# Hybrid decoder trunk: two score blocks ahead of the first gate part in the mixer's written order, other pieces moved by one place, input blocks in other tiles

## The chip, the cores and the metric

The kernel runs on one core of a Trainium2 chip. Its engines are TensorE (PE, matrix products into PSUM), VectorE (DVE) and ScalarE (ACT), GpSimd (POOL) and SyncE (SP), which here issues most DMA transfers. Each engine works through its own instruction queue in order and waits on semaphores of the others. The metric is the device time of one execution in microseconds (us), the median of the runs; lower is better.

## The reference

A two-layer decoder trunk on one sequence of 512 tokens and 1024 channels. Layer 0 mixes tokens with a diagonal state-space model (S5) on half of the projected channels and with stick-breaking attention (8 heads of 64) on the rest. Layer 1 is a convolution module. Each layer ends with a feed-forward net. The change touches the mixer of layer 0 alone:

```python
h = x @ mix_w_in[i] + mix_b_in[i]
u, q, k, v = jnp.split(h, [S5_WIDTH, S5_WIDTH + SB_WIDTH, S5_WIDTH + 2 * SB_WIDTH], axis=-1)
s5_out = s5_mixer(u, ...)
sb_out = stick_breaking_attention(q.reshape(head_shape), k.reshape(head_shape), v.reshape(head_shape))
mix = jnp.concatenate([s5_out, sb_out], axis=-1) @ mix_w_out[i] + mix_b_out[i]

# stick_breaking_attention, for each block of 128 queries
z = jnp.einsum('bqhd,bkhd->bhqk', q_blk, kf) * scale
log_beta = jax.nn.log_sigmoid(z)
log_keep = jnp.where(strict, jax.nn.log_sigmoid(-z), 0.0)
after = lax.cumsum(log_keep, axis=3, reverse=True) - log_keep
weights = jnp.where(strict, jnp.exp(log_beta + after), 0.0)
out = jnp.einsum('bhqk,bkhd->bqhd', weights, vf)

# s5_mixer: bu = u times b_bar, a causal scan of complex states, then
y = jnp.real(jnp.einsum('blgn,gpn->blgp', states, c))
y = jax.nn.gelu(y + d * u)
val, gate = jnp.split(y @ w_glu + b_glu, 2, axis=-1)
return val * jax.nn.sigmoid(gate)
```

## The kernel before

**Numbers.** Each large product is split into three: weights and inputs are cut into a high part (`whi`, `xh`, made by ACT) and a low part (`wlo`, `xl`, made by DVE as the difference), and PE multiplies high by high, high by low and low by high. A weight piece of 128 x 1024 numbers comes by DMA into `raw` (two buffers), then ACT casts it (L117 or L114) and DVE subtracts (L118 or L115). Three pieces may be ready at a time.

**Start.** Eight blocks of the input, `xin0` to `xin7`, are loaded into tiles that later serve others (tags "spt", "wt", "q", "k"), and PE turns them. Then come the four projections u0 to u3. Each leaves PSUM by an ACT copy `ue` (L652) into a tile of tag "wt" and goes through DRAM into `U`. Meanwhile ACT and DVE compute four sine and cosine tables (`tables`, L505 to L522): ACT writes `fa` and `fb`, DVE reduces them in four steps (L390, L514, L515, L390 and L517), and ACT takes Sin, Abs and Sin (`ts`, `fb`, `tc`). After the last Sin ACT loads another table set, for Exp and Ln.

**The mixer's order.** From there PE follows the list `ORDER` (L62): each word names a piece, and every PE instruction is tied behind the one before it (L844). DVE's, ACT's and SP's queues are not written by hand; the framework's scheduler puts them together from that program and its priorities. The words are:

- `q0`, `k0`, `v0` and so on: projections of 24 products of 512 columns, one pair of heads each. An ACT copy takes each out of PSUM.
- `G0` to `G3` (`s5_tables`): the gate part of the S5 model. DVE builds `Gx` and `Cx`; PE turns `Gx` (`gp`, two blocks) and multiplies (`tp`); ACT copies these out as `gt`, `gt` and `tk`; sixteen small DMA transfers put `tk` into `Tx`.
- `s0` to `s3` (`s5_states`): PE multiplies `vR` and `vI` from `gt` and `U`, DVE forms the states with the tables and two scans and writes `Sx`.
- `y0` to `y3` (`s5_outputs`): PE makes `yp` from `Tx`, `Cx` and `Sx`, and DVE adds it to `U` in four pieces. `Cx` for the next part may be written only when `yp` has read it.
- `a0sB`: score block B of head pair 0 (`z0B`, both heads), followed by its softplus: ACT takes Abs, Exp and Ln, DVE finishes `sp`, ACT casts `sh`, DVE subtracts `sl`. C and A likewise; C is half as wide.
- `a0t`: v0 turned (`vt`, copied out by ACT). `a0wB0`: the weights of block B, head 0, 8 products on `z0B`, and an Exp on ACT (`w0B`). `a0vC`: the values of block C, into the one buffer "av". `a0e`: that buffer is taken out (`ch` by ACT, `cl` by DVE), which frees it for the next pair.
- `e0`: the GELU of part 0. `r`, `R`: rows of bias vectors. `l0`, `o0`: the gated linear unit and the output product.

**Buffers.** In PSUM three buffers of tag "mm" go round over the projections, `gp`, `gp`, `tp`, `vt`, `vR`, `vI` and `yp` in the order of the program, so each of these waits until the third one back has been read; four of tag "z" hold scores, one "av". In SBUF the tiles "spt" and "wt" have three buffers each, "q" and "k" two.

Of the kernel before, what the change touches and what calls it, by code (L numbers as in the profile page):

```python
# [12 lines left out]
AF = mybir.ActivationFunctionType  # L13
# [43 lines left out]
MIX_BUFS = (3, 4, 1, 3, 3)  # L57
WARM = 24
QK_BUFS = (2, 2, 1, 1)
SP_BUFS = {"A": 1, "B": 2, "C": 2}  # L60
TABLES_FIRST = (0, 1, 2, 3)
ORDER = "q0 k0 v0 G0 s0 a0sB a0sC a0t q1 k1 y0 a0wB0 a0wC0 a0wC1 a0wB1 a0sA a0vC r G1 s1 a0wA0 v1 a0wA1 a0vB a1sC a1sB y1 q2 a0vA a1wC0 a1wC1 e0 G2 a1sA s2 k2 a1wB0 a0e a1t v2 a1wB1 a1vC y2 a1vB e1 a1wA0 a2sB a1wA1 q3 a1vA a1e e2 G3 a2sC s3 k3 a2wB1 a2t a2wC0 a2wC1 a2vC a2sA a2wB0 R y3 e3 v3 a3sC a2wA0 a2vB a2wA1 a3sB l0 a2vA a2e a3wC0 a3wC1 l1 a3t a3sA a3wB1 l2 l3 a3wA0 a3vC a3wB0 a3wA1 o0 o1 o2 o3 o4 o5 a3vB a3vA a3e o6 o7".split()  # L62


class Weights:
# [100 lines left out]
def units_of(name, w, k0, nk, cols, width):  # L166

    ncol = 1024 // nk
    out = []
    for c in cols:  # L170
        base = c // width * width
        src = w[k0 * P : (k0 + nk) * P, base : base + width].rearrange("(k p) n -> p k n", p=P)
        out.append(((name, k0, base), src, nk, ncol, c - base, width))
    return out
# [29 lines left out]
def kernel(ctx: ExitStack, tc: tile.TileContext, a: dict, out: bass.AP):  # L204
    nc = tc.nc
    act = Act(tc)
# [42 lines left out]
    def pv(n, i):  # L249
        if n == "mix_b_in":  # L250
            return PB[:, i : i + 1]
        return PV[:, vrow[n] + i : vrow[n] + i + 1]
# [25 lines left out]
    units = units_of("u", w_in, 0, 8, range(0, 512, 128), 128)  # L278
    for o in ORDER:
        if o[0] in "qkv":  # L280
# [38 lines left out]
    xin = []  # L319
    with tc.high_priority():  # L320
        for j in range(KT):
            tag, bufs = (("spt", MIX_BUFS[3]), ("wt", MIX_BUFS[4]), ("q", QK_BUFS[0]), ("k", QK_BUFS[1]))[(0, 1, 0, 1, 0, 1, 3, 2)[j]]
            xt = att.tile([P, 4, P], F32, tag=tag, name=f"xin{j}", bufs=bufs)
            nc.sync.dma_start(xt, a["x"][0][:, P * j : P * (j + 1)].rearrange("(b p) f -> p b f", p=P))
            xin.append(xt)
# [26 lines left out]
    for j in range(KT):  # L352
        ps = (mm if j % 2 else s5ps)(f"xT{j}")
# [275 lines left out]
    def c_states(last):  # L629
        with tc.issue_after(last):  # L630
            for i in range(2):
                cp = zz(f"cp{i}")
                for b in range(4):
                    PE.transpose(cp[:, b * P : (b + 1) * P], Craw[i][:, b, :], ident)
                cv = cp.rearrange("p (r g q) -> p r g q", g=2, q=16)
                for h in range(2):
                    hp = slice(h * 64, h * 64 + 64)
                    V.tensor_copy(Cd[hp, i], cv[hp, :, h, :])

    def in_proj(tile_i, name):  # L640
        w = W.next()
        ps = mm(name)
        proj_last[:] = [gemm(ps, w, slice(0, P), xs, 0, T)]
        return ps, pv("mix_b_in", tile_i)

    Ud = [tc.dram_tile([P, T], F32, name=f"Ud{j}") for j in range(4)]
    for j in range(4):
        ps, b = in_proj(j, f"u{j}") if j else (u0, pv("mix_b_in", 0))
        if j == 1:
            c_states(proj_last[0])  # L650
        up = att.tile([P, T], F32, tag="wt", name=f"ue{j}", bufs=MIX_BUFS[4])
        act(up.rearrange("p (t c) -> p c t", t=4), ps.rearrange("p (c t) -> p c t", t=4), AF.Identity, bias=b)  # L652
        nc.sync.dma_start(Ud[j], up)
        for t in range(4):
            nc.sync.dma_start(U[32 * t : 32 * t + 32, 4 * j : 4 * j + 4, :],
                              Ud[j].rearrange("(r f) (t c) -> t f r c", r=4, t=4)[t])
# [177 lines left out]
    before, traced = None, nc.cur_bb.bb.instructions  # L834
    for o in ORDER:
        at = len(traced)
# [64 lines left out]
    for layer in range(2):  # L901
# [3 lines left out]
        k0 = 0  # L905
# [200 lines left out]
    for n in ("ln1_g", "ln2_g", "conv_ln_g"):  # L1106
        c = PV[:, vrow[n] : vrow[n] + a[n].shape[0] * KT]
# [31 lines left out]
    k0 = 0  # L1139
# [90 lines left out]
    ws, ps, last = [None] * KT, [None] * KT, {}  # L1230
# [129 lines left out]
    def rect(m, ps):  # L1360

        r = page(f"r1{m}", F32)
        act(r, ps, AF.Relu, bias=pv("ffn_b1", 32 + m))
        return r

    def hidden(m):

        ps = stp(f"f1{m}")
        gemm(ps, W.next(), slice(0, P), xs, 0, T)
        return ps  # L1370
# [49 lines left out]
    k0 = 0  # L1420
# [9 lines left out]
    for i in range(nb_last):  # L1430
        if i % 3 == 0:
            hl_ = [f1[f"a{i // 3}"].tile([P, 3, T], F32R, tag=f"a{x}", name=f"b{x}{i}", bufs=1) for x in "hl"]
        r = rect(k0 + i, hidden(k0 + i))
# [88 lines left out]
```

## Time and profile before

| What | Value |
|---|---|
| median of 3 runs | 1146.21 us (1146.03 to 1146.39) |
| the profiled execution | 1147.06 us |
| its span, from first to last instruction | 1145.3 us |
| mean granted TensorE clock | 0.997 |
| four projections u, from the first product | 8.2 to 34.6 us |
| the mixer's written order | 34.4 to 232.7 us |
| DVE busy in 40 to 60 us | 19.56 of 20 us |
| ACT busy in 40 to 60 us | 15.37 of 20 us |

Rows of the timeline give start, duration, engine, line, operation, output and inputs, shapes and, in square brackets, how long the engine was idle before it and what ended that. A matmul's duration contains its way through the array, so rows overlap, and the distance of two starts says more than a duration. In the table of waits each row is one engine and operation, what it waited for, the total, the number of waits and the longest.

### The profile page before, as it was taken

The numbers are of one execution on the slowest core, as the hardware profiler recorded it, in microseconds if no ns is written. First come the engines' busy times: TensorE is split into PE (matmuls) and PEld (weight loads), VectorE is DVE, ScalarE is ACT, GpSimd is POOL, SyncE is SP. The second block draws the span as 40 slices with busy tenths as digits, with TensorE's granted clock in tenths as the row PEclk, the third lists the DMA queues.
The fourth block names the chain that finished last, engine by engine and source line by source line (L and its number), as shares of the span: only waits on it lengthen the run. The fifth ranks groups of instructions, "written<-read, shape, count | busy, mean of one in ns | idle before, by whom it ended". The sixth has DMA issues, their size and how long they took to land.

```text
span 1145.3 us, 16443 instructions
## 1 busy us (share of the span) xinstructions
PE 1124.8 (98%) x6460; PEld 945.5 (83%) x6460; DVE 811.6 (71%) x1408; ACT 538.7 (47%) x814; POOL 39.7 (3%) x77
## 2 busy tenths in 40 slices
PE   9999999999999999999999999999999999999997
PEld 7777777799887888888899887699988888888885
DVE  7998875588745644645547899877795959588337
ACT  6966778435524524524513321354674535363530
POOL 1000000000000000000002211002000000000000
PEclk9999999999999999999999999999999999999999
DMA  9621221150878778788608586546043241515211
GB/s 206 172 66 49 73 70 66 58 181 32 269 242 281 245 255 292 267 277 303 228 6 290 205 252 197 163 121 221 1 129 93 84 136 45 158 37 159 72 46 74
DMA packets 152109, 175.35 MB, mean 153 GB/s; under 512 B 15522, under 2 KB 124834, under 8 KB 152032
## 3 DMA queue, kind: packets, MB, share of 16 engines
q1 hardware_dynamic: 143232, 142.81, 39.4%
q0 software_dynamic: 8640, 31.46, 8.1%
q8 instruction: 51, 0.84, 0.3%
q14 instruction: 26, 0.21, 0.1%
q10 hardware_dynamic: 160, 0.03, 0.0%
HBM read 132.25 MB, written 35.65 MB: 147 GB/s over the span
## 4 chain that ended last, share of the span: by engine, by line
PE 88%; DVE 4%; DMA 4%; ACT 3%; issue 1%; SPq 0%; DVEq 0%; ACTq 0%
PE f L265 24%; PE acf L265 11%; PE s L1407 10%; PE fl L265 6%; PE tlb L265 4%; PE tld L265 4%; PE h L1452 4%; PE pv L265 3%; PE pg L265 3%; PE cw L1200 2%; PE tla L265 2%; PE pl L265 2%; PE v L265 1%; PE acmo L265 1%; DMA raw<-in_mix_w_in_dram 1%; PE gg L265 1%
## 5 line engine op out<-in xcount | busy, mean ns | idle before, releaser
L117 ACT CAST whi<-raw 128x1024 fp32r<-128x1024 f32 (+1 forms) x150 | 157.1, 1061 | 261.3 <-PE acf L265 72.5
L118 DVE TENSOR_TENSOR wlo<-raw,whi 128x1024 fp32r<-128x1024 f32 (+1 forms) x150 | 183.9, 1237 | 120.8 <-ACT whi L117 120.5
L265 PE MATMUL f<-xah,whi 128*128 128x512 f32 x208 | 81.1, 390 | 0.0
L265 PE MATMUL f<-xal,whi 128*128 128x512 f32 x208 | 81.0, 390 | 0.0
L265 PE MATMUL f<-xah,wlo 128*128 128x512 f32 x208 | 80.9, 389 | 0.0
L265 PE MATMUL f<-xdh,whi 128*128 128x512 f32 x208 | 80.9, 389 | 0.0
L265 PE MATMUL f<-xdl,whi 128*128 128x512 f32 x208 | 80.9, 389 | 0.0
L265 PE MATMUL f<-xdh,wlo 128*128 128x512 f32 x208 | 80.9, 389 | 0.0
L265 PE MATMUL acf<-hh,whi 128*128 128x512 f32 x192 | 76.0, 396 | 0.0
L265 PE MATMUL acf<-hh,wlo 128*128 128x512 f32 x192 | 75.6, 394 | 0.0
L265 PE MATMUL acf<-hl,whi 128*128 128x512 f32 x192 | 75.1, 391 | 0.0
L1407 PE MATMUL s<-whi,al 128*128 128x512 f32 x168 | 65.0, 390 | 0.0
L1407 PE MATMUL s<-wlo,ah 128*128 128x512 f32 x168 | 65.0, 390 | 0.0
L1407 PE MATMUL s<-whi,ah 128*128 128x512 f32 x168 | 64.5, 392 | 0.0
L118 DVE TENSOR_TENSOR wlo<-quad,whi 128x1536 fp32r<-128x1536 f32 x28 | 49.1, 1755 | 7.6 <-ACT whi L117 7.3
L117 ACT CAST whi<-quad 128x1536 fp32r<-128x1536 f32 x28 | 41.0, 1483 | 17.2 <-PE f L265 8.0
L398 DVE SCALAR_TENSOR_TENSOR cy<-hp,wdw,cy 128x256 f32<-128x256 f32 (+1 forms) x80 | 46.2, 578 | 0.4 <-ACT cy L192 0.4
L265 PEld LDWEIGHTS f<-xal,whi 128*128 128x128 f32 x208 | 39.0, 188 | 8.1
L265 PEld LDWEIGHTS f<-xdh,wlo 128*128 128x128 f32 x208 | 39.0, 188 | 8.1
L265 PEld LDWEIGHTS f<-xdh,whi 128*128 128x128 f32 x208 | 39.0, 188 | 8.1
L265 PEld LDWEIGHTS f<-xah,wlo 128*128 128x128 f32 x208 | 39.0, 188 | 8.1
L265 PEld LDWEIGHTS f<-xdl,whi 128*128 128x128 f32 x208 | 39.0, 188 | 8.1
(649 smaller groups left out, 2979.4 us busy)
## 6 DMA issues: line engine op xcount, KB each, us to landing
raw<-in_ffn_w_dram SPq DMA_DIRECT2D x35, 1024.0 KB, 5.4
kepth<-whi SPq DMA_DIRECT2D x30, 512.0 KB, 2.8
keptl<-wlo SPq DMA_DIRECT2D x30, 512.0 KB, 3.7
whi<-kepth POOLq DMA_DIRECT2D x30, 512.0 KB, 4.2
wlo<-keptl POOLq DMA_DIRECT2D x30, 512.0 KB, 5.3
raw<-in_ffn_w_dram SPq DMA_DIRECT2D x28, 512.0 KB, 3.9
raw<-in_conv_w_pw_dram SPq DMA_DIRECT2D x12, 1024.0 KB, 7.3
quad<-in_ffn_w_dram SPq DMA_DIRECT2D x16, 768.0 KB, 4.2
```

The costliest lines, as they stand in the source:

```text
L117: i0 = nc.scalar.copy(hi, raw).ins
L118: i1 = nc.vector.tensor_sub(lo, raw, hi.bitcast(F32)).ins
L265: ins = PE.matmul(ps[:, c0:c1], u[:, k, ksl], v[:, c0:c1], start=start and k == 0 and i == 0, stop=stop and k == n - 1 and i == 2).ins
L398: V.scalar_tensor_tensor(o, x, s, y, op0=op0, op1=op1)
L1200: PE.matmul(cps[j, c0][32 * g : 32 * g + 32, c0:c1], Ws[j][:, 4 * b + g, :], Hs[j, c0][g][:, 4 * b : 4 * b + c1 - c0], start=b == 0, stop= ...
L1407: PE.matmul(ps, u, v[:, p, :], start=chain == i and p == 0 and n_ == 0, stop=p == len(As) - 1 and n_ == 2, skip_group_check=True)
L1452: PE.matmul(ps, u, v, start=k == 0 and i == 0, stop=k == nb_last - 1 and i == 2)
```

## The change

Three edits. The list `ORDER` is changed in six places: the score blocks `a0sB a0sC` go ahead of `G0`, and `a0t` ahead of `s0`; `v1` goes ahead of `s1` and `a0wA0`; `q2` ahead of `y1`; `a0e` directly behind `a0vA`; and in the third pair `a2vC` goes behind `a2sA a2wB0`. Of the line the diff shows what moves. The input blocks use other tile tags. The ACT copy `ue` gets the scheduler's high priority.

```diff
-ORDER = "q0 k0 v0 G0 s0 a0sB a0sC a0t q1 k1 y0 a0wB0 a0wC0 a0wC1 a0wB1 a0sA a0vC r G1 s1 a0wA0 v1 a0wA1 a0vB a1sC a1sB y1 q2 a0vA a1wC0 a1wC1 e0 G2 a1sA s2 k2 a1wB0 a0e a1t v2 a1wB1 a1vC y2 ... a2wB1 a2t a2wC0 a2wC1 a2vC a2sA a2wB0 R y3 ..."
+ORDER = "q0 k0 v0 a0sB a0sC G0 a0t s0 q1 k1 y0 a0wB0 a0wC0 a0wC1 a0wB1 a0sA a0vC r G1 v1 s1 a0wA0 a0wA1 a0vB a1sC a1sB q2 y1 a0vA a0e a1wC0 a1wC1 e0 G2 a1sA s2 k2 a1wB0 a1t v2 a1wB1 a1vC y2 ... a2wB1 a2t a2wC0 a2wC1 a2sA a2wB0 a2vC R y3 ..."
@@ the input blocks @@
-            tag, bufs = (("spt", MIX_BUFS[3]), ("wt", MIX_BUFS[4]), ("q", QK_BUFS[0]), ("k", QK_BUFS[1]))[(0, 1, 0, 1, 0, 1, 3, 2)[j]]
+            tag, bufs = (("spt", MIX_BUFS[3]), ("k", QK_BUFS[1]), ("q", QK_BUFS[0]), ("wt", MIX_BUFS[4]))[(0, 1, 0, 1, 0, 2, 2, 3)[j]]
@@ the projections u @@
-        act(up.rearrange("p (t c) -> p c t", t=4), ps.rearrange("p (c t) -> p c t", t=4), AF.Identity, bias=b)
+        with tc.high_priority():
+            act(up.rearrange("p (t c) -> p c t", t=4), ps.rearrange("p (c t) -> p c t", t=4), AF.Identity, bias=b)
```

Lines behind L652 stand one further down in the changed kernel. Numbers behind the names are buffers; the same tile can have another one in the changed program.

The first place is DVE's queue at the end of the sine tables, from the low part of q1's weights (`wlo_720`) to the last step of the fourth table (`fa_508`, L517). Before:

```order
L115 SCALAR_TENSOR_TENSOR wlo_720<-raw_717,whi_719 128x1024
L390 TENSOR_SCALAR fr_510<-fa_508 128x512
L394 TENSOR_TENSOR cm<-EE,Braw 128x256
L517 TENSOR_TENSOR fa_508<-fa_508,fr_510 128x512
L394 TENSOR_TENSOR cm<-EE,Braw 128x256
L394 TENSOR_TENSOR Gx<-cm 64x16x16 x2
L394 TENSOR_TENSOR cm<-PW,Cd 128x320 x2
L394 TENSOR_TENSOR Cx<-cm 64x20x16 x2
L118 TENSOR_TENSOR wlo_753<-raw_750,whi_752 128x1024
```

And in the changed kernel, where `fa_487` is the third table:

```order
L115 SCALAR_TENSOR_TENSOR wlo_720<-raw_717,whi_719 128x1024
L515 TENSOR_TENSOR fa_487<-fa_487,fb_488 128x512
L390 TENSOR_SCALAR fr_510<-fa_508 128x512
L390 TENSOR_SCALAR fr_489<-fa_487 128x512
L514 TENSOR_TENSOR fa_508<-fa_508,fr_510 128x512
L517 TENSOR_TENSOR fa_487<-fa_487,fr_489 128x512
L515 TENSOR_TENSOR fa_508<-fa_508,fb_509 128x512
L394 TENSOR_TENSOR Cx<-cm 64x20x16
L390 TENSOR_SCALAR fr_510<-fa_508 128x512
L394 TENSOR_TENSOR cm<-PW,Cd 128x320
L118 TENSOR_TENSOR wlo_753<-raw_750,whi_752 128x1024
L517 TENSOR_TENSOR fa_508<-fa_508,fr_510 128x512
```

The steps of the third and fourth table, which stood ahead of `wlo_720`, now stand behind it, and the last one also behind `wlo_753`; the `cm`, `Gx` and `Cx` work moved ahead instead.

The second place is ACT's queue from its table load to the copies of the first gate part (`gt`, `gt`, `tk`) and of the turned v0 (`vt`). Before:

```order
L194 ACT_TABLE_LOAD
L117 CAST whi_938<-raw_936 128x1024
L192 ACTIVATE v_781<-v_756,PB 128x512
L565 COPY gt_808<-gp_803 128x512
L565 COPY gt_815<-gp_810 128x512
L577 COPY tk_826<-tp_817 128x128
L192 ACTIVATE sp0B_886<-z0B_876 128x512
L192 ACTIVATE sp0B_896<-z0B_877 128x512
```

In the changed kernel, from v0's copy to the first of these copies and on to the second:

```order
L192 ACTIVATE v_781<-v_756,PB 128x512
L192 ACTIVATE sp0B_793<-z0B_783 128x512
L192 ACTIVATE sp0B_803<-z0B_784 128x512
L198 ACTIVATE sp0B_793<-sp0B_793 128x512
L198 ACTIVATE sp0B_803<-sp0B_803 128x512
L198 ACTIVATE sp0B_793<-sp0B_793 128x512
L198 ACTIVATE sp0B_803<-sp0B_803 128x512
L192 ACTIVATE sp0C_818<-z0C_812 128x256
L565 COPY gt_861<-gp_856 128x512
L255 CAST sh0B_799<-sp0B_793 128x512
L255 CAST sh0B_808<-sp0B_803 128x512
L198 ACTIVATE sp0C_818<-sp0C_818 128x256
```

The queue goes on there with:

```order
L565 COPY gt_868<-gp_863 128x512
L198 ACTIVATE sp0C_818<-sp0C_818 128x256
L192 ACTIVATE sp0C_827<-z0C_813 128x256
L577 COPY tk_879<-tp_870 128x128
L198 ACTIVATE sp0C_827<-sp0C_827 128x256
L255 CAST sh0C_823<-sp0C_818 128x256
L198 ACTIVATE sp0C_827<-sp0C_827 128x256
L700 COPY vt_902<-vt_897 128x512
```

The softplus of the two score blocks, which followed `tk`, now stands between v0's copy and the four copies.

The third place is DVE's queue around `yp1`, the second S5 output, up to the last `Cx` of the third part. Before:

```order
L394 TENSOR_TENSOR Cx<-cm 64x20x16
L398 SCALAR_TENSOR_TENSOR sp1B_1278<-z1B_1268,sp1B_1278 128x512
L398 SCALAR_TENSOR_TENSOR sp1B_1287<-z1B_1269,sp1B_1287 128x512
L398 SCALAR_TENSOR_TENSOR U<-U,par,yp_1296 128x128
L256 TENSOR_TENSOR sl1B_1284<-sp1B_1278,sh1B_1283 128x512
L256 TENSOR_TENSOR sl1B_1293<-sp1B_1287,sh1B_1292 128x512
L398 SCALAR_TENSOR_TENSOR U<-U,par,yp_1296 128x128 x3
L394 TENSOR_TENSOR Cx<-cm 64x20x16
L394 TENSOR_TENSOR cm<-PW,Cd 128x320 x2
L398 SCALAR_TENSOR_TENSOR Cx<-cm 64x20x16 x2
```

In the changed kernel, where `wlo_1502` is the low part of q3's weights and `cl_1349` that of pair 0's values:

```order
L398 SCALAR_TENSOR_TENSOR sp1B_1287<-z1B_1269,sp1B_1287 128x512
L115 SCALAR_TENSOR_TENSOR wlo_1502<-raw_1499,whi_1501 128x1024
L256 TENSOR_TENSOR sl1B_1293<-sp1B_1287,sh1B_1292 128x512
L394 TENSOR_TENSOR Cx<-cm 64x20x16
L398 SCALAR_TENSOR_TENSOR U<-U,par,yp_1329 128x128 x4
L256 TENSOR_TENSOR cl_1349<-av_1075,ch_1348 128x512
L394 TENSOR_TENSOR Cx<-cm 64x20x16
L394 TENSOR_TENSOR cm<-PW,Cd 128x320 x2
L398 SCALAR_TENSOR_TENSOR Cx<-cm 64x20x16 x2
```

The softplus of the second pair stood behind the first `Cx`, and now stands ahead of it, with the weights; `cl` has come in.

More of the change, by code (lines that the diff above doesn't have):

```diff
@@ L61 @@
 TABLES_FIRST = (0, 1, 2, 3)
-ORDER = "q0 k0 v0 G0 s0 a0sB a0sC a0t q1 k1 y0 a0wB0 a0wC0 a0wC1 a0wB1 a0sA a0vC r G1 s1 a0wA0 v1 a0wA1 a0vB a1sC a1sB y1 q2 a0vA a1wC0 a1wC1 e0 G2 a1sA s2 k2 a1wB0 a0e a1t v2 a1wB1 a1vC y2 a1vB e1 a1wA0 a2sB a1wA1 q3 a1vA a1e e2 G3 a2sC s3 k3 a2wB1 a2t a2wC0 a2wC1 a2vC a2sA a2wB0 R y3 e3 v3 a3sC a2wA0 a2vB a2wA1 a3sB l0 a2vA a2e a3wC0 a3wC1 l1 a3t a3sA a3wB1 l2 l3 a3wA0 a3vC a3wB0 a3wA1 o0 o1 o2 o3 o4 o5 a3vB a3vA a3e o6 o7".split()
+ORDER = "q0 k0 v0 a0sB a0sC G0 a0t s0 q1 k1 y0 a0wB0 a0wC0 a0wC1 a0wB1 a0sA a0vC r G1 v1 s1 a0wA0 a0wA1 a0vB a1sC a1sB q2 y1 a0vA a0e a1wC0 a1wC1 e0 G2 a1sA s2 k2 a1wB0 a1t v2 a1wB1 a1vC y2 a1vB e1 a1wA0 a2sB a1wA1 q3 a1vA a1e e2 G3 a2sC s3 k3 a2wB1 a2t a2wC0 a2wC1 a2sA a2wB0 a2vC R y3 e3 v3 a3sC a2wA0 a2vB a2wA1 a3sB l0 a2vA a2e a3wC0 a3wC1 l1 a3t a3sA a3wB1 l2 l3 a3wA0 a3vC a3wB0 a3wA1 o0 o1 o2 o3 o4 o5 a3vB a3vA a3e o6 o7".split()
 class Weights:
```

## The prediction

> **What bounds the kernel now.** I read the page first, then the list of what TensorE waited for, then engine timelines of the first 160 us, where every step of the change lies. All times are us from the start of the span unless a clock or a count is meant.
>
> ```profile
> PE 1124.8 (98%) x6460; PEld 945.5 (83%) x6460; DVE 811.6 (71%) x1408; ACT 538.7 (47%) x814; POOL 39.7 (3%) x77
> PE 88%; DVE 4%; DMA 4%; ACT 3%; issue 1%; SPq 0%; DVEq 0%; ACTq 0%
> ```
>
> The page says that TensorE (PE) is the bound: 98% busy, and 88% of the chain that ended last. Behind the mixer there is almost no idle time on it, so whatever shift the mixer has gathered when it ends arrives unchanged at the end of the span. The question is only how the mixer's PE queue shifts. PE works strictly in the written order there, so each of its waits counts in full.
>
> ```profile
> PE vR L588 <- ACT gt L565: 1.9, 1, 1.9
> PE tp L573 <- issue: 1.5, 1, 1.5
> PE v L265 <- ACT ue L192: 1.3, 1, 1.3
> PE av L760 <- DVE cl L256: 0.9, 1, 0.9
> PE av L760 <- ACT w2C L198: 0.9, 2, 0.5
> ```
>
> These five rows of the waits (engine, line, what it waited for; total, times, longest) are what the change can hope to take: 6.5 us in all. The opposite danger is in the table of windows, where VectorE (DVE) is full as well:
>
> ```profile
> 40.00:60.00 20.00, 17.26 (x106) 13.48 (x106) 19.56 (x37) 15.37 (x28) 0.99 (x1) 1.00 0.53 140
> ```
>
> The columns are stretch, length, busy time of PE, weight loads, DVE, ACT and POOL, then clock and DMA. DVE is busy 19.56 us of 20, and ACT and PE feed it. An order that lets DVE or ACT stand still here cannot be made good soon.
>
> **The wait for ue3, and what is late next.** The three "mm" buffers of PSUM go round, so v0 takes the one of u3 and waits until ScalarE (ACT) has copied ue3 out.
>
> ```profile
> 51.10 0.68 ACT L192 ACTIVATE k<-k,PB 128x512 f32<-128x512 f32 x1
> 54.83 0.73 PE L573 MATMUL tp<-Cx,Gx 128*32 128x128 f32 x16 [1.48 <-issue]
> 57.46 1.14 PE L718 MATMUL z0B<-q,k 64*128 64x384 f32 x8
> 60.03 0.62 PE L697 MATMUL vt<-ident,v 128*128 128x128 f32 x4
> 60.41 0.47 PE L265 MATMUL q<-x0h,whi 128*128 128x512 f32 x1
> ```
>
> With its high priority ue3 comes out several us before v0 asks for it, so v0 starts and ends 1.3 earlier. But behind v0 now stand the score blocks z0B and z0C, which read k0 from SBUF. ACT copies k0 out at 51.10 to 51.78, and in the new order no earlier, since that copy stands behind the third table's Sin. So z0B starts near 52.0, and most of the 1.3 comes back at once. The two score blocks (57.46 to 60.03, 2.6) then end near 54.6, the gate transposes gp near 55.6.
>
> **Trig tables later (the DVE place of the change section).** DVE's last subtraction for the fourth table (L517) is what ACT's last Sin waits for.
>
> ```profile
> 45.82 1.22 DVE L115 SCALAR_TENSOR_TENSOR wlo<-raw,whi 128x1024 fp32r<-128x1024 f32 x1
> 46.96 0.42 DVE L390 TENSOR_SCALAR fr<-fa 128x512 f32<-128x512 f32 x1
> 47.63 0.69 DVE L517 TENSOR_TENSOR fa<-fa,fr 128x512 f32<-128x512 f32 x1
> ```
>
> Now it follows wlo_720 by two rows; in the new order by ten. A row's length from start to start is its duration less some 0.09 (wlo: 1.22, but the next begins 1.14 later; fr and cm: 0.67 for the two). The ten are four of L517's kind at 0.60, three fr of 0.33, one Cx of 0.5, one cm of 0.45 and the whole of wlo_753 (1.14), together 5.5. The work ahead of wlo_720 is the same within some 0.3 us, so I leave that at 45.82: 45.82 + 1.14 + 5.5 + 0.69 = 53.1 for the end of L517, where it was 48.3.
>
> ```profile
> 48.35 0.64 ACT L198 ACTIVATE ts<-fa 128x512 f32<-128x512 f32 x1 [0.64 <-DVE fa L517]
> 50.16 1.03 ACT L117 CAST whi<-raw 128x1024 fp32r<-128x1024 f32 x1
> 51.80 1.28 ACT L194 ACT_TABLE_LOAD   x1
> 54.04 0.68 ACT L192 ACTIVATE v<-v,PB 128x512 f32<-128x512 f32 x1
> 54.62 1.06 ACT L565 COPY gt<-gp 128x512 f32<-128x512 f32 x2
> 55.62 0.27 ACT L577 COPY tk<-tp 128x128 f32<-128x128 f32 x1
> 59.12 1.09 ACT L192 ACTIVATE sp0B<-z0B 128x512 f32<-128x512 f32 x2 [3.24 <-PE z0B L722]
> 60.09 2.19 ACT L198 ACTIVATE sp0B<-sp0B 128x512 f32<-128x512 f32 x4
> 62.17 0.38 ACT L192 ACTIVATE sp0C<-z0C 128x256 f32<-128x256 f32 x1
> 62.44 0.60 ACT L699 COPY vt<-vt 128x512 f32<-128x512 f32 x1
> 62.91 0.90 ACT L198 ACTIVATE sp0C<-sp0C 128x256 f32<-128x256 f32 x2
> 68.39 1.22 ACT L255 CAST sh0B<-sp0B 128x512 fp32r<-128x512 f32 x2 [4.59 <-DVE sp0B L398]
> ```
>
> From ts to the end of tc ACT needs 1.9 (48.35 to about 50.25); whi_752 and k, which stood behind, now stand ahead of that. The table load therefore starts at 53.1 + 1.9 = 55.0 instead of 51.80, and v0's copy ends 2.9 later (51.80 to 54.72 now), at 57.9 instead of 54.7. PE's tp needs that copy's buffer, so tp goes from 54.83 to 57.9; since the score blocks are done by then, nothing is lost yet.
>
> **The gate's copies behind the softplus (the ACT place): term A.** Now gt, gt, tk follow v at once. After the change 3.3 us of softplus stand between v and the first gt, and all the rest between v and vt: sp0B Abs 0.97, four Exp and Ln 2.08, sp0C Abs 0.27, gt 0.50, two casts 1.13, Exp 0.43, gt 0.50, Ln 0.43, Abs 0.27, tk 0.27, Exp 0.43, cast 0.29, Ln 0.43, vt 0.47, each from start to start in the rows above (0.29 is an estimate for the cast of a half block, half of 0.57): 8.5 us. DVE, which those casts need, has run out of work there and follows within that sum. PE has three "mm" buffers: vt waits for the first gt, vR for the second, vI for tk, and q1 for the copy of vt, at 57.9 + 8.5 = 66.4. It starts at 60.41 now. **A = +6.0.** ACT's idle 3.24 and 4.59 in the rows above are used up, but they cost PE nothing: no row of its waits names the z0B or z0C weights, which need this softplus. If the tables kept their time (v0 out at 54.7), A would be 63.2 - 60.4 = +2.8; half a microsecond of further slip gives +6.6.
>
> ```profile
> 57.51 10.33 SPq L580 DMA_DIRECT2D Tx<-tk  x16
> ```
>
> The sixteen Tx transfers that tk lets go move with it: tk is out near 64.8, SP issues until 75.1, and yp0, their reader, comes some 11 us after q1, near 77.5 or later. They stay hidden with 2 us or so to land in; if they landed late, each us would add to A.
>
> **The clock: term B.**
>
> ```profile
> 82.00:84.00 2.00, 1.27 (x9) 1.27 (x10) 1.99 (x5) 1.85 (x5) 0.00 (x0) 0.90 0.00 0
> 84.00:86.00 2.00, 2.00 (x12) 2.00 (x11) 1.97 (x4) 0.00 (x0) 0.00 (x0) 0.50 0.06 16
> 86.00:88.00 2.00, 2.00 (x10) 1.82 (x10) 1.38 (x3) 0.54 (x2) 0.00 (x0) 0.74 0.13 31
> ```
>
> After the 1.9 us wait of vR the granted clock falls to 0.90, 0.50 and 0.74; 2 us at each loses 0.2 + 1.0 + 0.5 = 1.7. The 1.26 and 1.48 waits lost nothing. In the new order PE is idle for some 7 of the 11 us ahead of q1, so I add one more such drop, taken at **B = +1.5**; with none it is 0, with another at tp2 (below) 3.4. The drop at 84 stays, since v1, put there, waits for the same gt copy. The Trainium skill, "TensorE: Matmul & The Clock Gate", Part 1, has the clock fall to half after at least one idle window of about 3.4 us and stay there until a busy one; by that a drop costs up to 1.7. The rows agree on the half and on the size, though here a wait of 1.9 sufficed.
>
> **v1 ahead of vR1: term C.** PE's work is the same. DVE now has wlo_1299 ahead of the products of vR1, and must wait for whi after v1; the last z0A products wait for sl0A behind them. v1's end to sl0A: whi 1.05, wlo 1.14, three products and sl0A itself at 0.6, together 4.6.
>
> ```profile
> 111.29 1.16 PE L588 MATMUL vR<-U,gt 128*128 128x128 f32 x8
> 92.97 0.22 PE L745 MATMUL z0A<-sh0B,negs 128*128 128x128 f32 x1
> 94.34 1.08 PE L760 MATMUL av<-w0B,vt 128*64 128x384 f32 x8
> ```
>
> PE has in between vR and vI, 1.0 each, and both heads' z0A weights, 1.37 each (92.97 to 94.34): 4.7. So it is nearly even; I take **C = +0.3**, between 0 and 0.7.
>
> **yp1 behind q2: term D (the DVE place at yp1).** Cx for the third part may only be overwritten once yp1 has read it, and tp2 reads it.
>
> ```profile
> 106.21 1.08 PE L760 MATMUL av<-w0A,vt 128*64 128x512 f32 x4
> 108.24 1.03 PE L563 MATMUL gp<-ident,Gx 128*128 128x128 f32 x8
> 109.20 0.64 PE L573 MATMUL tp<-Cx,Gx 128*32 128x128 f32 x16
> 105.95 0.49 DVE L394 TENSOR_TENSOR Cx<-cm 64x320 f32<-64x320 f32 x1
> 107.41 0.99 DVE L398 SCALAR_TENSOR_TENSOR Cx<-cm 64x320 f32<-64x320 f32 x2
> ```
>
> Today the last Cx ends at 108.40, 0.8 ahead of tp, and all of q2 lies between yp1 and tp2. With q2 moved ahead, PE has only av, the z1C weights and gp left: 106.21 to 109.20, 3.0 us. DVE needs Cx 0.5, four U (128 columns each; 1.1 is an estimate from the half microsecond of 320 columns), cl 0.6 (moved there too), then Cx, two cm and two Cx as from 105.95 to 108.40, 2.4: 4.6. The wait is 1.6 at least, and 3.4 if DVE is still at wlo_1502 and sl1B (1.8) when yp1 ends, which I expect, as DVE has stood idle for several us on the way. **D = +3.0.**
>
> **What is gained: terms E and F.** cl0 now comes early, so the 0.9 of av behind cl goes: **E = -0.9**. The a2 C values behind z2A and z2B lose their 0.9, but w2C1 moves behind five softplus rows of 0.5 us on ACT: between -0.9 and +0.5, **F = 0**. The other tile tags of the input blocks cost nothing: PE has read them all by 14, before any new owner writes.
>
> **Sum.** 6.0 + 1.5 + 0.3 + 3.0 - 0.9 + 0 = +9.9. The profiled execution took 1147.06 (span 1145.3 and 1.8 around it), 0.85 over the median of the runs; 1156.96 there, 1156.1 as a median.
>
> **Rivals.**
> - Faster. The waits for ue3, v0's copy, cl and w2C go (1.26 + 1.48 + 0.9 + 0.9 = 4.5) and nothing replaces them: 1146.2 - 4.5 = 1141.7. It decides at one place: gt must be copied by the end of the new gp and tp, about 56, so v0 must leave ACT by 52.2. For it: DVE and ACT have the idle time shown. Against: the load, whi and v alone take 2.9 from a start that is 51.80 even now. Chance 0.06.
> - The loss is only the queue on ACT: tables on time (A = 2.8), no further clock drop, D at 1.6, E in full: +3.5, 1149.7, from 1148.5 to 1152. For it: the table delay is worked out over many rows. Chance 0.17.
> - No change: the softplus done earlier gives back at z0B's weights what q1 lost. Against: those have no wait in the list of waits, there is nothing to give back. 1146, chance 0.05.
>
> **How the numbers follow.** My forecast, +6 to +14, has 0.72. The range takes the ends: 2.8 + 0 + 0 + 1.6 - 0.9 - 0.9 = +2.6 gives 1148.8, and 6.6 + 3.4 + 0.7 + 3.4 + 0 + 0.5 = +14.6 gives 1160.8. It leaves out the two cases at or below no change and a little of the third. Slower by over 0.2% (2.3 us, about what a measurement of this kernel can tell) has 0.72 + 0.17 = 0.89, faster 0.06.
>
> **What would show it.** In the new profile: no wait of v for ue; z0B near 52; the table load near 55; q1 near 66 behind waits for gt and vt; a low clock around 60 to 70; tp2 waiting for Cx; av not waiting for cl. I am wrong if the table load stays near 52, or if the first gt is copied before the softplus.

## The result and the profile after

| | before | after |
|---|---|---|
| median of 5 runs each | 1146.39 us (1146.03 to 1148.13) | 1158.25 us (1155.66 to 1161.24) |
| ratio of the runs | | 1.0099, 95% interval 1.0086 to 1.0112 |
| the profiled execution | 1147.06 us | 1155.66 us |
| its span, granted clock | 1145.3 us, 0.997 | 1154.0 us, 0.993 |

The change makes the kernel 1% slower: some 12 us by the medians, 8.6 between the two profiled executions. The profiled one of after is the lowest of its five runs. Of all runs in this document one was slow, a run of e10 below with 1590.47 us at a granted clock of 0.654, and the ratios leave it out. The page of after shows no other bound; TensorE is as busy as before:

```profile
PE 1127.9 (98%) x6460; PEld 947.5 (82%) x6460; DVE 811.9 (70%) x1408; ACT 538.6 (47%) x814; POOL 39.5 (3%) x77
PE 88%; DVE 4%; ACT 4%; DMA 3%; issue 1%; DVEq 0%; SPq 0%; ACTq 0%
```

The loss is in the list of what PE waited for in the first 175 us (engine, line, what it waited for; total, times, longest):

```profile
PE vt L698 <- ACT gt L565: 3.1, 1, 3.1
PE tp L573 <- issue: 2.3, 1, 2.3
PE v L265 <- ACT gt L565: 1.9, 1, 1.9
...
PE tp L573 <- DVE Cx L398: 1.5, 1, 1.5
PE av L761 <- ACT w2C L198: 1.3, 1, 1.3
PE tp L573 <- DVE Cx L394: 1.0, 1, 1.0
PE vR L588 <- ACT gt L565: 0.7, 1, 0.7
PE z0B L719 <- ACT k L192: 0.6, 1, 0.6
PE z0A L746 <- DVE sl0A L256: 0.5, 1, 0.5
```

Of the five waits that the prediction began with, the one for ue3 and the one for cl are gone. The gate's 1.9 now stands at v1 instead of vR, tp's 1.5 has become 2.3, and the one for w2C stays with 1.3. New are 3.1 and 0.7 behind the first gate copies, 0.6 for k, 0.5 for sl0A, and 2.5 of tp for Cx. For the wait of 2.3 the profile names no releaser ("issue"); it is read as the wait for v0's copy, since tp starts 0.1 behind the end of that copy in before, after, e1 and e8 alike (54.72 and 54.83, 57.27 and 57.37 in the first two). ACT's timeline of after shows the first gate part:

```profile
48.75 0.63 ACT L198 ACTIVATE ts<-fa 128x512 f32<-128x512 f32 x1 [1.70 <-DVE fa L517]
...
52.42 0.63 ACT L198 ACTIVATE ts<-fa 128x512 f32<-128x512 f32 x1 [0.37 <-DVE fa L517]
...
54.34 1.28 ACT L194 ACT_TABLE_LOAD   x1
...
56.59 0.68 ACT L192 ACTIVATE v<-v,PB 128x512 f32<-128x512 f32 x1
...
60.46 0.60 ACT L565 COPY gt<-gp 128x512 f32<-128x512 f32 x1
...
62.29 0.61 ACT L565 COPY gt<-gp 128x512 f32<-128x512 f32 x1
...
63.34 0.31 ACT L577 COPY tk<-tp 128x128 f32<-128x128 f32 x1
...
64.54 0.56 ACT L700 COPY vt<-vt 128x512 f32<-128x512 f32 x1
```

ACT stands still for 1.70 until DVE hands over the third table, the table load starts at 54.34 instead of 51.80, and v0 leaves PSUM at 57.27 instead of 54.72. The three gate copies, which followed at once in before, are strewn over the softplus, and the copy of vt, for which q1 did not wait in before, ends at 65.10. On PE that gives

```profile
62.95 2.08 PE L588 MATMUL vR<-U,gt 128*128 128x128 f32 x8 [0.72 <-ACT gt L565]
...
66.38 0.76 PE L265 MATMUL q<-x0h,whi 128*128 128x512 f32 x1
```

q1 starts 5.97 later than the 60.41 of before. Its first product takes 0.76, and from vR to vI it is 1.86 instead of 1.00, since the clock is at half, as the windows of after show (the columns are those of the prediction: busy time of PE, weight loads, DVE, ACT, POOL, then clock, DMA share and GB/s):

```profile
60.00:62.00 2.00, 0.88 (x4) 0.71 (x4) 1.96 (x5) 2.00 (x6) 0.00 (x0) 0.54 0.63 188
62.00:64.00 2.00, 1.28 (x7) 1.05 (x6) 2.00 (x5) 2.00 (x8) 0.00 (x0) 0.50 0.00 0
64.00:66.00 2.00, 2.00 (x11) 2.00 (x11) 1.15 (x3) 1.10 (x3) 0.00 (x0) 0.50 0.06 16
66.00:68.00 2.00, 2.00 (x10) 1.73 (x10) 2.00 (x6) 0.41 (x1) 0.00 (x0) 0.75 0.09 23
...
88.00:90.00 2.00, 1.01 (x4) 0.86 (x5) 2.00 (x5) 2.00 (x5) 0.00 (x0) 1.00 0.00 0
...
118.00:120.00 2.00, 2.00 (x9) 0.50 (x6) 1.85 (x6) 1.55 (x2) 0.00 (x0) 0.55 0.18 40
120.00:122.00 2.00, 2.00 (x12) 2.00 (x13) 1.55 (x4) 1.68 (x4) 0.00 (x0) 0.59 0.44 101
```

Before had one such stretch, from 83.6 to 87.0. After has two others, ahead of q1 and behind tp of the third part, and none behind v1's wait.

### The profile page after: what moved, and what is told of

It is laid out like the page before. It is cut to its first block, busy times and chain, and to the rows that moved or that the text cites. A ratio compares the mean times of both kernels' runs of the same rounds, so it can differ in the third digit from the quotient of the medians.

```text
span 1154.0 us, 16441 instructions
## 1 busy us (share of the span) xinstructions
PE 1127.9 (98%) x6460; PEld 947.5 (82%) x6460; DVE 811.9 (70%) x1408; ACT 538.6 (47%) x814; POOL 39.5 (3%) x77
## 4 chain that ended last, share of the span: by engine, by line
PE 88%; DVE 4%; ACT 4%; DMA 3%; issue 1%; DVEq 0%; SPq 0%; ACTq 0%
PE f L265 24%; PE acf L265 11%; PE s L1408 10%; PE fl L265 6%; PE tlb L265 4%; PE tld L265 4%; PE h L1453 4%; PE pv L265 3%; PE pg L265 3%; PE cw L1201 2%; PE tla L265 2%; PE acmo L265 2%; PE pl L265 2%; PE v L265 1%; PE k L265 1%; DMA raw<-in_mix_w_in_dram 1%
```

## The experiments

Each kernel was timed beside runs of before on the same chip. Besides the ratio, one number of each profile is used: the start of the first output product (`acmo`, piece o0), 207.65 in before. It leaves out what differs behind the mixer, where nothing was changed: from there to the end of the span it was 936.9 to 940.5 us. The table sums up; the shifts are against the profile of before.

| kernel | q1 starts | acmo starts | ratio to before, 95% interval |
|---|---|---|---|
| after | +5.97 | +9.07 | 1.0099 (1.0086 to 1.0112) |
| e5 after once more | +6.48 | +9.74 | 1.0084 (1.0069 to 1.0099) |
| e1 ue priority alone | +5.25 | +4.45 | 1.0050 (1.0036 to 1.0063) |
| e2 head of the order alone | +3.07 | +2.86 | 1.0028 (1.0016 to 1.0039) |
| e3 after without ue priority | +2.97 | +6.61 | 1.0063 (1.0050 to 1.0075) |
| e4 after with the old head | +5.76 | +8.55 | 1.0083 (1.0068 to 1.0098) |
| e6 after with y1 back | +6.43 | +10.61 | 1.0089 (1.0073 to 1.0106) |
| e7 after with v1 back | +5.92 | +7.66 | 1.0078 (1.0060 to 1.0096) |
| e8 ue priority and tables early | +2.17 | +2.07 | 1.0018 (1.0008 to 1.0029) |
| e9 after with v1 and y1 back | +6.33 | +6.39 | 1.0062 (1.0044 to 1.0081) |
| e10 gate copies of part 1 first | -0.07 | -2.59 | 0.9971 (0.9960 to 0.9983) |
| e11 the same and a0e early | +0.24 | -2.32 | 0.9977 (0.9968 to 0.9986) |
| e12 head alone, its copies early | -0.35 | +0.42 | 1.0013 (1.0003 to 1.0023) |

Part of a shift is the clock. Between 10 us and acmo the clock column has 3.4 us at half clock in before, 6.8 in e1, e2, e8 and e9, 10.2 in after, e3, e4 and e7, 13.7 in e5 and e6, and none in e10 to e12; each 3.4 cost up to 1.7.

The tiles of the input blocks were not run apart. But e1 and e4, and e2 and e3, differ only in them and in the later moves, and in both pairs PE, DVE and ACT have the same instructions in the same order up to the first of those moves (v1 at 88.50 in e4, at 86.64 in e3).

### Which edit costs what: e1 to e4

e1 is before with the third edit alone:

```diff
-        act(up.rearrange("p (t c) -> p c t", t=4), ps.rearrange("p (c t) -> p c t", t=4), AF.Identity, bias=b)
+        with tc.high_priority():
+            act(up.rearrange("p (t c) -> p c t", t=4), ps.rearrange("p (c t) -> p c t", t=4), AF.Identity, bias=b)
```

> Before, with the high priority of the ue copies alone (the written order and the tiles of before). By my theory the priority is no help: it moves the third and fourth sine tables behind other work on DVE and ACT, so the table load starts near 54.3 instead of 51.80 and v0's copy ends near 57.2 instead of 54.72. v0 on PE starts 1.3 earlier, the two gp end near 52.1, and tp then waits some 5 us for that copy; q1 starts near 62.4 instead of 60.41 (+2.0), and one drop of the granted clock may add 1.5. Time +2.0 to +3.6 over before: a ratio of 1.0017 to 1.0031. By the rival (the wait for ue3 simply goes, and the head of the order alone is to blame) it is -1.3 or no change, ratio 0.999 to 1.000, with the table load still near 52.

The direction was right and the size too small: 1152.42 us, +5.7, a ratio of 1.0050 where 1.0017 to 1.0031 was expected. Two rows of ACT's and two of PE's timeline:

```profile
55.21 1.28 ACT L194 ACT_TABLE_LOAD   x1
...
57.45 0.68 ACT L192 ACTIVATE v<-v,PB 128x512 f32<-128x512 f32 x1
```

```profile
58.23 0.44 PE L573 MATMUL tp<-Cx,Gx 128*32 128x128 f32 x4 [5.22 <-issue]
...
65.66 0.47 PE L265 MATMUL q<-x0h,whi 128*128 128x512 f32 x1
```

v0 starts without a wait for ue3, and the time comes back, and more, as one wait of 5.22 that ends behind v0's copy (58.13). tp is 3.4 late (54.83 before), and from tp to q1 it takes 7.43 instead of 5.58, because the clock is at half from 55.6 to 62.4. The edit that removes the wait for ue3 is alone the costliest part of the change.

e2 is before with the first move alone, `q0 k0 v0 a0sB a0sC G0 a0t s0 q1` for `q0 k0 v0 G0 s0 a0sB a0sC a0t q1`.

> Before, with only the two score blocks and a0t moved ahead in the head of the written order. ACT's queue in front of v0's copy is as before, so the table load should stay at 51.8 and v0's copy end at 54.7; behind it stand 8.5 us of softplus and gate copies up to the copy of vt. By my theory q1 starts at 54.7 + 8.5 = 63.2 instead of 60.41: +2.8, and up to 1.5 more if the clock drops on the way: ratio 1.0024 to 1.0038. By the rival that the softplus is only done earlier and nothing is lost, ratio 1.000. By the rival that the head alone makes the whole loss, +6 or more, ratio over 1.005.

1150.30 us, +3.6, as the theory had it. ACT's rows of the four copies and PE's q1:

```profile
57.79 0.60 ACT L565 COPY gt<-gp 128x512 f32<-128x512 f32 x1
...
59.62 0.61 ACT L565 COPY gt<-gp 128x512 f32<-128x512 f32 x1
...
60.66 0.31 ACT L577 COPY tk<-tp 128x128 f32<-128x128 f32 x1
...
61.87 0.57 ACT L699 COPY vt<-vt 128x512 f32<-128x512 f32 x1
```

```profile
63.48 0.48 PE L265 MATMUL q<-x0h,whi 128*128 128x512 f32 x1
```

vt is out at 62.44, and q1 starts at 63.48 instead of the expected 63.2, held back by vR and vI at half clock (59.8 to 63.2).

e3 is after without the `with tc.high_priority():` around ue, e4 is after with the old head, `q0 k0 v0 G0 s0 a0sB a0sC a0t q1`.

> The changed kernel without the high priority of the ue copies. By my theory the tables come early again (table load near 51.8), so term A is 2.8 instead of 6.0 and q1 starts near 63.2 instead of 66.4; the rest of the change (yp1 behind q2, v1 ahead of vR1, a0e, a2vC; +2.7 together in the profiled pair) stays. Time +5 to +6 over before, that is 3 less than the changed kernel: ratio to before 1.0045 to 1.0055. If the clock drops ahead of q1 are the main loss and follow from the head of the order, it stays within 1.5 of the changed kernel: ratio 1.008 or more.

> The changed kernel with the head of the written order as before (gate part and states ahead of the score blocks); ue priority and all later moves stay. By my theory the late tables alone are left at the head: q1 near 62.4 (+2.0, up to +3.6 with a clock drop) instead of 66.4, and the later moves add 2.7: +4.7 to +6.3 over before, ratio 1.004 to 1.0055. By the rival that the head's order makes the whole of term A, q1 is back at 59 to 60.4 and the sum is +2.7 or less: ratio 1.0025 or less.

e3 took 1153.81 us, 1.0063, a little over what was expected: q1 at +2.97 as in e2, so term A does fall to 3 without the late tables. e4 missed: 1156.06 us, 1.0083, hardly less than after. The old head does not help, since e1's wait of 5.2 is then there in full (q1 at +5.76). Head and tables do not add at q1: +3.07 and +5.25 apart, +5.97 together, because the score blocks fill 2.6 us of the wait that the late tables make. The moves further down add 3.75 (6.61 - 2.86) or 4.10 (8.55 - 4.45) at acmo, where 2.7 was expected; in both pairs one more 3.4 us at half clock is part of it.

### Why the ue priority costs time: e8

e8 is e1 with the tables under the same priority:

```diff
-        tables(q)
+        with tc.high_priority():
+            tables(q)
```

> Before, with the high priority of the ue copies and the same high priority for the code of the four sine tables; the written order is that of before. It tests why the ue priority alone cost 5.7 us. By my theory the ue copies do no harm by themselves; they let DVE's and ACT's queues put the third and fourth table behind other work, and v0's copy, behind the table load, comes 2.9 to 3.4 us later. With the tables ahead again, the load is back at 52 or earlier, the 5.2 us wait of tp shrinks to 3 or less without a half clock behind it, and the time is within 1.5 of before: ratio 0.998 to 1.0015. By the rival that ue's place on ACT, or the transfers that it starts, cost the time, the ratio stays at 1.004 to 1.006.

1149.43 us, 1.0018: by the ratios about two thirds of e1's loss go, by the medians half (+2.75 of +5.70). The ratio is a little over the expected 1.0015, and its interval reaches into that range; the rival's 1.004 is out. ACT's table load and the first rows of what PE waited for:

```profile
52.57 1.28 ACT L194 ACT_TABLE_LOAD   x1
...
54.82 0.68 ACT L192 ACTIVATE v<-v,PB 128x512 f32<-128x512 f32 x1
```

```profile
PE tp L574 <- issue: 2.3, 1, 2.3
PE vR L589 <- ACT gt L566: 1.9, 1, 1.9
```

With the load at 52.57, v0's copy ends at 55.50, 0.8 later than in before. So most of the harm is not in the place of the ue copies but in the tables that they pushed back. The load is not quite back at 52, and 0.8 of q1's shift of +2.17 is that. What was expected too well is the rest: no half clock. PE is idle here about as long as in before ahead of tp (0.6 for k and 2.3, against 1.26 and 1.48), but closer together, and the clock is at half from 55.4 to 58.8. That the rest of the loss is this stretch is read from the profile, not tried.

### The softplus in front of the gate copies: e12

e12 is e2, and the copies gt, gt and tk of part 0 and vt of pair 0 have the high priority:

```diff
-            S.copy(g_, gp.rearrange("p (r c) -> p r c", r=4))
+            with tc.high_priority() if q == 0 else ExitStack():
+                S.copy(g_, gp.rearrange("p (r c) -> p r c", r=4))
...
-        S.copy(tk, tp[:, :P])
+        with tc.high_priority() if q == 0 else ExitStack():
+            S.copy(tk, tp[:, :P])
...
-            S.copy(vt, vps.rearrange("p (b c) -> p b c", b=4))
+            with tc.high_priority() if p == 0 else ExitStack():
+                S.copy(vt, vps.rearrange("p (b c) -> p b c", b=4))
```

> The written order's head alone, as in the second kernel (before with a0sB a0sC ahead of G0 and a0t ahead of s0; 1.0028 there), and the copies gt, gt, tk of part 0 and vt of pair 0 under high priority. In ACT's queue they now stand behind v0's copy, both Abs and three Exp and Ln, with one cast before vt, instead of being strewn over 8.5 us of softplus. Term A says that this queue and nothing else made q1 late: from v0's copy at 54.6 the gt copies come at 57.1 and 57.6, tk at 58.1, vt near 59.0 to 59.6, and q1 starts near 60.5, where it started at 63.48 in that kernel and at 60.41 in before: ratio 0.9995 to 1.001. By the rival that the score blocks cost PE time by their place, or that the softplus, now later, is missed at the z0B weights, the loss stays: 1.002 or more.

```profile
57.12 1.08 ACT L566 COPY gt<-gp 128x512 f32<-128x512 f32 x2
58.07 0.30 ACT L579 COPY tk<-tp 128x128 f32<-128x128 f32 x1
...
58.74 0.63 ACT L702 COPY vt<-vt 128x512 f32<-128x512 f32 x1
```

```profile
60.06 0.48 PE L265 MATMUL q<-x0h,whi 128*128 128x512 f32 x1
```

PE's written order is that of e2. ACT's queue differs, and from 57.8 on DVE's with it. vt is out at 59.37 instead of 62.44, and q1 starts at 60.06 instead of 63.48: 2.0 of the 3.4 are waits for gt (one of 1.21, against 2.02 and 1.17), the rest is the half clock that e2 had there. That settles term A's mechanism: what made q1 late is not the place of the score blocks on PE, but the softplus that came in front of four copies.

The place is not free, though. The score blocks put vR at 58.26, 2.8 later than in before, while yp0 stays where it was; DVE has the softplus among the steps of the states, and yp0 gets a wait that neither before nor e2 has:

```profile
72.53 1.00 PE L622 MATMUL yp<-Sx,Cx 128*128 128x128 f32 x4 [1.08 <-DVE Sx L394]
```

vR of part 1 is then 1.31 late (84.04). That acmo is nevertheless at +0.42 is the clock: the stretch at half clock that before has there is missing in this profile. The ratio, 1.0013, lies over the expected 0.9995 to 1.001, and its interval overlaps that of e2, so the times alone do not tell the two apart. The median of 1149.06 us is higher than its profiled run (1146.70, without any half clock); its twelve runs spread from 1146.70 to 1151.31. What the slower of them have was not profiled.

### The later moves: e5, e6, e7, e9

e5 is after once more.

> The changed kernel once more, beside the two kernels below and the same runs of before. Its runs so far spread from 1155.66 to 1161.24, three times as wide as those of before, and the one with a profile was the lowest: there the 1.9 us wait of v1 near 87 cost no drop of the clock, though the same length did in before near 82. If the spread is the clock's, a profile of a run near 1158 shows one stretch of about 3.4 us at half clock more than the first profile (there: one from 60 to 67, one from 118 to 122), worth 1.5 to 1.7. If it shows the same stretches and 1158, the spread comes from elsewhere. Ratio to before 1.009 to 1.011.

1157.25 us; the profiled run took 1157.06. The ratio, 1.0084, is a little under what was expected. The expected stretch behind v1 is not there. The one ahead of q1 is longer by a step, 57.6 to 67.8 instead of 60.2 to 67.0, but q1 loses only 0.5 by it; another 0.7 of the 1.4 us between the two profiled runs lies behind acmo. The spread is only partly the clock's.

e6 is after with `y1 q2` for `q2 y1`. e7 is after with `G1 s1 a0wA0 v1 a0wA1` for `G1 v1 s1 a0wA0 a0wA1`. e9 has both.

> The changed kernel with y1 q2 in their old order; a0e stays directly behind a0vA. By my theory of term D, Cx for the third part is ready before tp asks for it: the two waits of tp for DVE Cx (1.0 and 1.5) go, and with them the half clock of 118 to 122 (1.6): -2.5 to -4.1 against the changed kernel, ratio to before 1.006 to 1.008. By the rival that DVE is late there anyway (its queue runs behind since the head), the waits come back at gp or at the z1A products and no more than 1 us is won.

> The changed kernel with s1 and a0wA0 ahead of v1 again. Term C says: the wait of z0A for sl0A (0.5) goes, and vR takes over from v1 the wait for gt (1.9); if the half clock follows that wait as in before, 1.7 is lost that the changed order did not lose in its profiled run. Between -0.5 and +1.7 against the changed kernel, ratio to before 1.0085 to 1.0125. If moving v1 were a real part of the loss, it would gain 1 us or more.

> The changed kernel with both v1 and y1 in their old places (s1 a0wA0 v1, and y1 q2); the head, the ue priority, a0e directly behind a0vA and a2vC stay. Undone alone, y1 gave nothing, since with v1 still ahead of vR1 the states Sx come late and yp1 waited 3.0 us for them. If the two moves belong together, undoing both takes the wait of yp1 for Sx, of tp for Cx (2.5) and of z0A for sl0A (0.5) away at once, and the half clock near 118 to 122 with them, while vR waits 1.9 for gt as in before and the clock drops there: -2.5 to -3.5 against the changed kernel, ratio to before 1.0055 to 1.0075. If DVE is simply behind after the head, whatever the order, one of the waits stays and the ratio is 1.008 or more.

e6 missed: 1157.40 us, 1.0089, nothing gained. The waits for Cx are gone, but another one is at the top of its list:

```profile
PE yp L620 <- DVE Sx L394: 3.0, 2, 2.0
```

Neither theory had named it. With v1 ahead of vR1 the states of part 1 start one projection later on DVE, and yp1 at its old place waits for them. In the change q2 ahead of y1 covers that, and pays with Cx. e7 took 1155.91 us, 1.0078, less than the expected 1.0085 to 1.0125. Its interval overlaps that of after, but acmo is at +7.66, 1.4 less, which is on the side of the rival that moving v1 is a real part of the loss: vR waits 1.9 as in before, the wait for sl0A is gone, tp waits 1.9 for Cx instead of 2.5. e9 took 1155.12 us with acmo at +6.39, 2.7 to 3.4 less than after's two profiles, and its ratio is in the expected range, though partly by luck, since the half clock expected behind vR did not come. Neither the waits for Cx nor the one for sl0A nor the half clock near 118 is in its profile, and yp1 does not wait (yp2 does, 0.8 for Sx). The two moves have to be judged together.

### A version that beats both: e10, e11

The wait of 1.9 behind ACT's gt, which before and after share, is a queue on ACT as well: gt, gt and tk of part 1 stand behind four Exp and Ln of sp0A. e10 is before with

```diff
-            S.copy(g_, gp.rearrange("p (r c) -> p r c", r=4))
+            with tc.high_priority() if q == 1 else ExitStack():
+                S.copy(g_, gp.rearrange("p (r c) -> p r c", r=4))
...
-        S.copy(tk, tp[:, :P])
+        with tc.high_priority() if q == 1 else ExitStack():
+            S.copy(tk, tp[:, :P])
```

and `G1 s1 v1 a0wA0 a0wA1` in the order. e11 has in addition `a0vA a0e`, as in the change.

> Before, with the copies gt, gt and tk of the second gate part (part 1) under high priority, and v1 ahead of a0wA0 (s1 v1 a0wA0 a0wA1); nothing of the change. In ACT's queue these three copies now stand ahead of the four Exp and Ln of sp0A instead of behind. By the theory of the ACT queue, vR's wait of 1.9 us near 82 goes and with it the stretch at half clock behind it (1.7); v1's 5.6 us on PE cover the softplus that is 1.3 us later: -2 to -3.6, ratio to before 0.997 to 0.998, which would beat both kernels. By the rival that the wait moves to the z0A weights (softplus later by 1.3), 0 to -1: ratio 0.999 to 1.000.

> As the kernel before it in this list, and a0e directly behind a0vA, the one move of the change that the prediction counted as a gain (term E, -0.9: av no longer waits for cl). Expected: 0.9 less than that kernel, ratio to before 0.996 to 0.9975. If cl was late for a reason that lies on DVE and not in its place, no difference.

e10 took 1144.77 us, ratio 0.9971 (0.9960 to 0.9983): faster than before and, by the two ratios, 1.1 to 1.3% faster than after. ACT's timeline and the windows of e10:

```profile
79.94 1.09 ACT L566 COPY gt<-gp 128x512 f32<-128x512 f32 x2
80.88 0.32 ACT L579 COPY tk<-tp 128x128 f32<-128x128 f32 x1
81.04 2.24 ACT L198 ACTIVATE sp0A<-sp0A 128x512 f32<-128x512 f32 x4
```

```profile
82.00:84.00 2.00, 2.00 (x14) 1.74 (x13) 2.00 (x5) 1.28 (x3) 0.00 (x0) 1.00 0.10 25
84.00:86.00 2.00, 2.00 (x10) 1.65 (x9) 2.00 (x5) 0.62 (x1) 0.00 (x0) 1.00 0.09 23
```

Here PE had waited, and then run at half clock. Now it is busy throughout, and of the 3.6 us 0.9 come back as a wait of z0A for sl0A: acmo is at -2.59. The priority and the place of v1 were changed together, and what each is worth alone was not tried. e11 shows no gain by a0e early: 1145.52 us, 0.9977 where 0.996 to 0.9975 was expected, with an interval that overlaps e10's. In its profile av's wait for cl is gone, q3 has gained 0.34 on e10 since v2, and at k3 0.30 of that has been given back.

## Why the prediction was right, and which of its steps were not

The forecast was 1156.1 us, from 1148.8 to 1160.8, slower; measured were 1158.25 and, in the second set, 1157.25. The direction and the two engines that cause it were right. By its steps, with the profile of after:

- **z0B near 52, the load near 55.0:** 51.48 and 54.34. DVE was 0.7 earlier with the tables than worked out.
- **A = +6.0, q1 at 66.4:** q1 is at 66.38, but not by its working. That had vt's copy end at 66.4; it ends at 65.10, since v0's copy is 0.6 earlier (57.27) and the queue behind it takes 7.8 instead of 8.5. So the queue makes 4.7 (65.10 - 60.41), and the remaining 1.3 are vR and vI at half clock. Two errors cancelled at this row, so that it came out so closely is luck. The bound of 2.8 with the tables on time is near e2 and e3 (+3.07 and +2.97), but there too the queue alone makes less: 2.0 in e2 (62.44 - 60.41), and the half clock the rest.
- **B = +1.5, one more drop, and the old one at 84 stays:** the size held, the place did not. Ahead of q1 1.3 is lost and another 0.3 by the time k1 starts (+6.26). The old stretch is gone, which gives some 1.7 back, and a new one behind tp costs about 1.5. The net is +1.4.
- **C = +0.3:** the wait for sl0A is 0.5.
- **D = +3.0:** 2.5. k2's shift of +9.59 is made up of +6.26 at k1, 0.5 of C, 2.5 of D, the new stretch of 1.5 and the old one's -1.7, together 9.1; 0.5 of it stays unassigned.
- **E = -0.9:** q3's shift is +8.70, 0.9 less. e11 shows that such a gain need not last.
- **F = 0:** pvp, the next product behind a2's values, is at +9.56, so F costs 0.9 there; 0.5 comes back before acmo (+9.07).

What the steps did not have at all: that the two causes of A overlap. The order of the text gave 2.8 to the softplus and 3.2 to the tables, to be added. Alone, the tables cost 5.25 at q1 and the softplus 3.07; of the 5.97 of both, undoing the head leaves 5.76, and undoing the priority 2.97. The edit that looked like help, ue's priority, is the larger one. And the 1.26 for ue3 was no loss of its own in before: ACT's rows there have v0's copy right behind the table load and whi, so it would not have come sooner with an earlier v0.

The rivals fall with the same runs. Faster, -4.5: e1 shows v's wait gone and 5.22 at tp in its place. No change by softplus done early: e2 does it early and loses 3.6. Loss by the queue alone, +3.5: its condition, tables on time, does not hold in after (the load is at 54.34), and e3, which lacks the priority that delays them, still loses 7.1.

## What to carry to other kernels

A priority given to one copy is taken from whatever stood next to it in the same queue: look at what moves back, and who waits for that, before counting the wait that goes. Where one engine's queue holds both a long chain (softplus, tables) and short copies that free PSUM, try the copies in front, and look at who then waits for the chain. In this kernel three copies put ahead of four activations, with v1 moved to cover the delay, won 0.3%, and softplus put ahead of four copies lost as much. In e12 the copies in front brought q1 back, but yp0 then waited for the states. Moves that cover each other, as v1 ahead of the states and q2 ahead of y1, must be undone together to be measured.

## What the runs showed of the hardware

The half clock comes in stretches of one length or a multiple of it. From half-microsecond windows of before (83.5 and 87.0) and of after, where the clock column tells how much of the half microsecond was at half:

```profile
83.50:84.00 0.50, 0.50 (x5) 0.50 (x4) 0.49 (x3) 0.35 (x2) 0.00 (x0) 0.61 0.00 0
...
87.00:87.50 0.50, 0.50 (x4) 0.41 (x3) 0.38 (x1) 0.04 (x1) 0.00 (x0) 0.97 0.09 23
```

```profile
60.00:60.50 0.50, 0.00 (x0) 0.00 (x0) 0.50 (x2) 0.50 (x3) 0.00 (x0) 0.68 1.14 345
67.00:67.50 0.50, 0.50 (x4) 0.42 (x3) 0.50 (x3) 0.00 (x0) 0.00 (x0) 0.99 0.04 10
...
118.00:118.50 0.50, 0.50 (x6) 0.31 (x4) 0.50 (x2) 0.37 (x2) 0.00 (x0) 0.71 0.00 0
121.50:122.00 0.50, 0.50 (x6) 0.50 (x6) 0.17 (x1) 0.50 (x2) 0.00 (x0) 0.88 0.61 140
```

A clock of 0.61 is 78% of 0.5 us at half, so before's stretch runs from 83.61 to 87.03: 3.42. After's run from 60.18 to 67.01 and from 118.21 to 121.62: 6.83 and 3.41, and their starts are 58.03 apart, 17 times 3.41. e5's first lasts 10.2. The same wait of 1.92 for gt is followed by a stretch in before, e2 and e8 and by none in after, e1, e3 to e7 and e9; e12's wait of 1.98 is followed by none either. Counting in steps of 3.41 from another stretch of the same profile, the wait lies inside one step in the first three; in after, e1 and e3 to e7 an edge cuts it (1.79 or less in the larger part), in e12 it leaves 1.63 in the larger part, and in e9 it begins 0.03 ahead of an edge. Idle time inside a step adds up: after's stretch from 118.21 follows waits of 1.02 and 1.52, of which 2.40 lie in the step ahead of it. That the edge decides is read from these profiles, not tried. The Trainium skill, "TensorE: Matmul & The Clock Gate", Part 1, has a free-running window of 3413 ns and re-throttling after at least one idle window; the lengths agree with the window, but a wait of 1.92, little more than half of one, was enough three times.

So a wait of some 2 us on PE cost the wait itself in one profile and up to 1.7 more in another. That more such waits make the times wider is not shown: in the first set after's five runs spread over 5.6 us and before's over 2.1, but in the second after's six over 2.0 and before's seventeen over 4.8.
